# Ordering the three matmuls of a split product by parts in a one-core transformer kernel

## The chip, the cores and the metric

The kernel runs on one core of one Trainium2 chip. The metric is device time in microseconds (us); lower is better. Three runs of the kernel before gave 1061.06, 1062.39 and 1064.32 us, a median of 1062.39 us. The profile is of one more execution, which took 1064.48 us.

## The reference, cut to what matters

A sequence of 256 tokens with model width 1024 goes through seven layers, all in float32: differential attention with a pooling mixer, a feed-forward layer with a short convolution, sliding-window attention, a second such feed-forward layer, a SwiGLU layer, a mixer of a 31-tap convolution and forgetting attention, and another SwiGLU layer. Every layer has a norm ahead of it and a residual behind it. What costs the time are the matrix products:

```python
proj = rms_norm(x, norm_g) @ w_in           # 1024 x 2048, 1024 x 1280, 1024 x 2568
x = x + mix @ w_out                         # 1024 x 1024, three times
h = rms_norm(x, norm_g) @ w_up              # 1024 x 5632, four times
x = x + (jax.nn.silu(gate) * up) @ w_down   # 2816 x 1024, four times
```

## The kernel before

**Products.** A float32 product is made of three matmuls of a rounded type. Activations and weights are each split into a first part (the rounded value, "hi") and a rest ("lo", what rounding took away): first by first, first by rest, and rest by first are summed in PSUM. One *block* is 128 rows of the contraction (index `ko`). With two token halves (`tb`, 128 tokens each) the activations stand as `xT` with a hi and a lo part.

There are three helpers. `mm3` (line 254, matmuls on lines 256 to 258) has activations as the stationary operand and weights as the moving one; it is called block by block from `rows_mm` (line 327), which `Proj.half`, `FFN.lead`, `OutProj.part` and `keys_C` use, and from `FFN.down` (line 428). `mm_w` (line 473, matmuls on lines 475 to 477) has weights stationary and 256 tokens moving; `conv_in` (line 1002), `forget_sums` (1056) and `proj_qk` (1089) call it once for each of the eight blocks. `mm_both` (line 479, matmuls on 483 and 485) makes the up-products of the feed-forward layers; it already goes by parts and isn't touched.

**Weights.** A `Stream` (line 174) loads weight chunks of 128 x 2048 in a written order through two staging tiles `st`. ScalarE casts the first part `whi` in two pieces (line 203), VectorE subtracts the rest `wlo` in four pieces of 512 columns (line 207). Five chunks are held at once. The splits have a priority that is 400 places behind the program's place (`LATER`, line 194). A chunk's buffers come free when the last matmul that reads them is done.

**Activations.** `split_T` (line 269) makes `xT` from transposes: ScalarE writes hi (line 274), then VectorE lo (line 275).

**Order.** The program is unrolled in Python. The order of the calls at lines 698 to 761, 886 to 960 and 1153 to 1224 is written by hand: products, scores, transposes and residuals of the three mixer layers are interleaved there. The tile layer then orders each engine's instructions by priority (the place in the program, with offsets such as `LATER`, and `LATERC = 300` for the convolution's rows on VectorE) and by what is ready, and puts in the semaphores. Each engine executes its instructions in that order.

In the last mixer layer `conv_in(3)` (line 1172) is followed by `proj_qk(1, 2)`, `proj_qk(1, 1)`, `proj_qk(0, 2)` and more (1174 to 1183). `proj_qk(1, ...)` reads the last two weight chunks of the stream for this layer. The 31-tap convolution runs on VectorE as `Conv.rows` (line 1030, instructions of line 1036), and `f1.scores` (line 1180) needs VectorE for line 586.

Of the kernel before, what the change touches and what calls it, by code (L numbers as in the profile page):

```python
# [18 lines left out]
P = 128  # L19
S = 256  # L20
D = 1024
KD = D // P
FF = 2816
NF = FF // P
# [84 lines left out]
def block_kernel(ctx: ExitStack, tc: tile.TileContext, a: dict, out: bass.AP):  # L109
    nc = tc.nc  # L110
    V, A, T, G = nc.vector, nc.scalar, nc.tensor, nc.gpsimd
# [114 lines left out]
    W = Stream()  # L226
# [24 lines left out]
    srow = const.tile([P, 280], F32, name="srow")  # L251
    nc.sync.dma_start(out=srow, in_=a["srow"].to_broadcast([P, 280]))

    def mm3(o, l, r, first, last):

        T.matmul(o, l[0], r[0], start=first, stop=False)  # L256
        T.matmul(o, l[0], r[1], start=False, stop=False)  # L257
        T.matmul(o, l[1], r[0], start=False, stop=last)  # L258

    def cut(pair, *idx):  # L260
        return tuple(t[idx] for t in pair)

    def tok(tb):
        return slice(tb * P, (tb + 1) * P)
# [61 lines left out]

    def rows_mm(o, xT, tb, w, kos, first, last, n0=0, n=512):

        for i, ko in enumerate(kos):
            mm3(  # L330
                o[:, :n], cut(xT, slice(None), ko, tok(tb)),
                cut(w, slice(None), i, slice(n0, n0 + n)),
                first and i == 0, last and i == len(kos) - 1,
            )

    def v3(pair, k):
        return tuple(t.rearrange("p (k n) -> p k n", k=k) for t in pair)

    class OutProj:
# [6 lines left out]
        def part(self, tb, *kks):  # L346
            if tb not in self.accs:
                self.accs[tb] = [acc_t(f"op{tb}{n}") for n in range(2)]
            for kk in kks:
                w = v3(W.get(self.wname, kk), 2)  # L350
                for n in range(2):
                    rows_mm(self.accs[tb][n], self.mixT, tb, w, (2 * kk, 2 * kk + 1),
                            self.done[tb] == 0, self.done[tb] == 3, n * 512)
                self.done[tb] += 1
                W.used(self.wname, kk)

# [4 lines left out]
    class FFN:  # L361
# [66 lines left out]
        def down(self, p, tb):  # L428
            if self.accs is None:
                self.accs = [[acc_t(f"dn{b}{n}") for n in range(2)] for b in range(2)]  # L430
            w = v3(W.get(self.dn, p), 2)
            for n in range(2):
                for i in range(2):
                    g = tuple(self.gs[p][:, i, k, tok(tb)] for k in range(2))
                    mm3(self.accs[tb][n], g, cut(w, slice(None), i, slice(n * 512, (n + 1) * 512)),
                        p == 0 and i == 0, p == NF // 2 - 1 and i == 1)
            W.used(self.dn, p)

        def run(self, pre, post, before=None, led=()):
# [30 lines left out]
        def residual(self, tb):  # L470
            add_residual(tb, self.accs[tb], 0.5 if self.half else None)

    def mm_w(o, w, xT, ko, first, last):
        x = cut(xT, slice(None), ko, slice(0, S))
        T.matmul(o, w[0], x[0], start=first, stop=False)
        T.matmul(o, w[0], x[1], start=False, stop=False)
        T.matmul(o, w[1], x[0], start=False, stop=last)

    def mm_both(o, ws, xT):

# [25 lines left out]
    xT = new_T("xT")  # L506
# [255 lines left out]
    xT = norm.dst  # L762
# [200 lines left out]
    xT = nT  # L963
# [38 lines left out]
    def conv_in(j):  # L1002
        ag[j] = ps_t("ag").rearrange("p (s t) -> p s t", s=2)
        w = v3(W.get("w2", j), KD)
        for s in range(2):
            for ko in range(KD):
                mm_w(ag[j][:, s, :], cut(w, slice(None), ko, slice(s * P, (s + 1) * P)),
                     xT, ko, ko == 0, ko == KD - 1)
        W.free(("w2", j))

    class Conv:
# [44 lines left out]
    def forget_sums():  # L1056

        o = ps_t("fl")[:8, :S]
        for ko in range(KD):
            mm_w(o, cut(flw, slice(None), ko), xT, ko, ko == 0, ko == KD - 1)  # L1060
        z, cum = (tmp.tile([P, S], F32, tag="sl", name=n)[:8, :] for n in ("z", "cum"))
        e = tmp.tile([P, S], F32, tag="m", name="e")[:8, :]
        A.activation(z, o, AF.Identity, bias=PVs("fb")[:8, :])
        V.scalar_tensor_tensor(e, z, -1.0, z, ALU.mult, ALU.min)
        A.activation(e, e, AF.Exp)
        A.activation(e, e, AF.Ln, bias=1.0)
        V.scalar_tensor_tensor(z, z, 0.0, e, ALU.min, ALU.subtract)
        V.tensor_tensor_scan(cum, one[:8, :].to_broadcast([8, S]), z, 0.0, ALU.mult, ALU.add)
        crow, ncrow = (u288(n, F32R)[:, :S] for n in ("crow", "ncrow"))
        V.memset(crow.bitcast(F32), 0.0)  # L1070
        A.copy(crow[0:8, :], cum)
        V.tensor_tensor(crow[32:40, :], cum, crow[0:8, :].bitcast(F32), ALU.subtract)
        V.tensor_scalar(ncrow, crow.bitcast(F32), -1.0, None, ALU.mult)
        gates["k"], gates["q"] = crow, ncrow
# [13 lines left out]

    def proj_qk(s, b):
        o = ps_t("qk")  # L1090
        for ko in range(KD):
            mm_w(o[:, :S], cut(v3(W.get("w2", 4 + 2 * s + ko // 4), 4), slice(None), ko % 4, slice(b * P, (b + 1) * P)),
                 xT, ko, ko == 0, ko == KD - 1)
        A.activation((q2, k2)[s][:, b, :], o[:, :S], AF.Copy, scale=1.0 if s else -0.125)
        if b == 3:
            W.free(("w2", 4 + 2 * s), ("w2", 5 + 2 * s))
# [222 lines left out]
```

## Time and profile before

| | |
|---|---|
| median of three runs | 1062.39 us (1061.06 to 1064.32) |
| the profiled execution | 1064.48 us |
| its span, first to last instruction | 1062.6 us |
| outside the span | 1.9 us |
| TensorE (PE) matmuls | 1038.6 us busy, 98% of the span, 5862 instructions |
| TensorE weight loads (PEld) | 895.1 us, 84%, 5862 instructions |
| VectorE (DVE) | 779.4 us, 73% |
| ScalarE (ACT) | 620.5 us, 58% |
| mean granted TensorE clock | 0.997 |

A busy matmul row lasts longer than the distance to the next one, because matmuls are pipelined: the rate is read from the start times. Four long stretches (126 to 299, 399 to 571, 582 to 757 and 889 to 1055 us) are the feed-forward layers; the first stretch, 299 to 399 and 757 to 889 us are the three mixer layers.

### The profile page before, as it was taken

The page shows a single profiled execution, that of the slowest core. Times are in us where ns is not written, and L with a number is a line of the kernel's source. Part 1 is how long each engine was busy: PE and PEld are TensorE (multiplying, and loading weights), DVE is VectorE, ACT ScalarE, POOL GpSimd, SP SyncE. Part 2 cuts the span into 40 slices and gives each one's busy share as a digit, 9 for nine tenths or more (in the row PEclk, how much of TensorE's full clock was granted, in tenths as well). Part 3 has the DMA queues.
Part 4 walks back from the last instruction along what each step waited for, and adds up shares of the span by engine and source line. Part 5 has one row for each costly group of instructions (what it writes and reads, how often), then busy time and mean ns, then how long its engine had stood idle before and what let it go on. Part 6 is the DMA issues. An engine that isn't in the chain of part 4 may idle for free.

```text
span 1062.6 us, 15441 instructions
## 1 busy us (share of the span) xinstructions
PE 1038.6 (98%) x5862; PEld 895.1 (84%) x5862; DVE 779.4 (73%) x1678; ACT 620.5 (58%) x1105; POOL 32.0 (3%) x40
## 2 busy tenths in 40 slices
PE   5999999999999999999999999999999999999997
PEld 4778988888887898888889888888898889888885
DVE  5786789788867579888787666656799896656652
ACT  5584666667657457766665555554644556555542
POOL 1100000000021000000000000000000010000000
PEclk9999999999999999999999999999999999999999
DMA  6654555655452064665545655554613166655531
GB/s 254 247 197 159 178 179 204 212 198 199 157 180 96 25 227 151 214 219 200 195 163 182 214 185 193 198 187 171 214 64 120 41 218 220 216 172 192 191 119 40
DMA packets 28442, 185.69 MB, mean 175 GB/s; under 512 B 3280, under 2 KB 4176, under 8 KB 7120
## 3 DMA queue, kind: packets, MB, share of 16 engines
q1 hardware_dynamic: 28368, 184.71, 50.1%
q8 instruction: 46, 0.75, 0.3%
q14 instruction: 28, 0.23, 0.1%
HBM read 183.65 MB, written 1.05 MB: 174 GB/s over the span
## 4 chain that ended last, share of the span: by engine, by line
PE 90%; DVE 3%; DMA 3%; ACT 2%; issue 0%; POOL 0%; SPq 0%; POOLq 0%; ACTq 0%; DVEq 0%
PE up L483 26%; PE up L485 13%; PE dn L256 8%; PE dn L257 8%; PE dn L258 7%; PE sc L583 2%; DMA st<-in_w 2%; PE op L256 2%; PE op L258 2%; PE op L257 2%; PE proj L256 2%; PE proj L258 2%; DVE wlo L207 2%; PE proj L257 2%; PE lead L258 2%; PE lead L257 2%
## 5 line engine op out<-in xcount | busy, mean ns | idle before, releaser
L207 DVE TENSOR_TENSOR wlo<-st,whi 128x512 fp32r<-128x512 f32 x668 | 433.4, 685 | 157.7 <-ACT whi L203 157.0
L203 ACT CAST whi<-st 128x1024 fp32r<-128x1024 f32 x334 | 338.7, 1048 | 136.8 <-PE dn L258 29.8
L483 PE MATMUL up<-xT,whi 128*128 128x512 f32 x1216 | 304.6, 392 | 1.4 <-DVE c L413 1.4
L483 PEld LDWEIGHTS up<-xT,whi 128*128 128x128 f32 x1216 | 220.6, 189 | 42.7 <-issue 1.8
L485 PEld LDWEIGHTS up<-xT,wlo 128*128 128x128 f32 x1216 | 165.9, 190 | 11.9
L485 PE MATMUL up<-xT,wlo 128*128 128x256 f32 x1216 | 169.6, 282 | 0.0
L256 PE MATMUL dn<-whi,g 128*128 128x512 f32 x352 | 137.7, 391 | 0.0
L257 PE MATMUL dn<-wlo,g 128*128 128x512 f32 x352 | 137.4, 390 | 0.0
L258 PE MATMUL dn<-whi,g 128*128 128x512 f32 x352 | 137.0, 389 | 0.0
L490 ACT COPY h<-up 128x256 f32<-128x256 f32 x152 | 55.8, 367 | 65.8 <-PE up L485 65.7
L258 PEld LDWEIGHTS dn<-whi,g 128*128 128x128 f32 x352 | 66.1, 188 | 14.3 <-DVE g L426 0.3
L256 PEld LDWEIGHTS dn<-whi,g 128*128 128x128 f32 x352 | 66.2, 188 | 12.9 <-ACT g L425 0.2
L257 PEld LDWEIGHTS dn<-wlo,g 128*128 128x128 f32 x352 | 66.2, 188 | 12.2
L425 ACT CAST g<-m 128x256 fp32r<-128x256 f32 x88 | 35.5, 405 | 60.9 <-DVE m L421 60.8
L491 DVE TENSOR_TENSOR h<-up,h 128x256 f32<-128x256 f32 x152 | 63.4, 417 | 9.6 <-ACT h L490 9.6
L256 PE MATMUL lead<-whi,xT 128*128 128x256 f32 x192 | 55.2, 288 | 0.0
L258 PE MATMUL lead<-whi,xT 128*128 128x256 f32 x192 | 54.3, 283 | 0.0
L257 PE MATMUL lead<-wlo,xT 128*128 128x256 f32 x192 | 54.3, 283 | 0.0
L410 ACT ACTIVATE c<-h,pv 128x256 f32<-128x256 f32 x76 | 45.8, 603 | 6.7 <-DVE h L491 6.6
L256 PE MATMUL proj<-whi,xT 128*128 128x512 f32 x112 | 46.2, 412 | 2.3 <-ACT xT L274 2.3
L426 DVE TENSOR_TENSOR g<-m,g 128x256 fp32r<-128x256 f32 x88 | 36.9, 422 | 14.7 <-ACT g L425 11.8
L284 ACT ACTIVATE junk<-x 128x512 bf16<-128x512 f32 x32 | 20.2, 631 | 44.6 <-DVE x L323 26.0
(215 smaller groups left out, 1389.2 us busy)
## 6 DMA issues: line engine op xcount, KB each, us to landing
st<-in_up SPq DMA_DIRECT2D x88, 1024.0 KB, 4.8
st<-in_dn SPq DMA_DIRECT2D x44, 1024.0 KB, 4.8
st<-in_w SPq DMA_DIRECT2D x22, 1024.0 KB, 4.8
gb<-in_rows SPq DMA_DIRECT2D x10, 512.0 KB, 4.3
st<-in_w0o SPq DMA_DIRECT2D x4, 1024.0 KB, 5.0
st<-in_w1o SPq DMA_DIRECT2D x4, 1024.0 KB, 4.8
st<-in_w2o SPq DMA_DIRECT2D x4, 1024.0 KB, 4.9
st<-in_w SPq DMA_DIRECT2D x2, 512.0 KB, 7.0
```

The source lines that it names most:

```text
L203: A.copy(hi[:, c], st[:, c])
L207: V.tensor_sub(lo[:, c], st[:, c], hi[:, c].bitcast(F32))
L256: T.matmul(o, l[0], r[0], start=first, stop=False)
L257: T.matmul(o, l[0], r[1], start=False, stop=False)
L258: T.matmul(o, l[1], r[0], start=False, stop=last)
L410: A.activation(c, ps, AF.Identity, bias=PVs(cb, blk), scale=PVs(cw, 3 * blk + 2))
L425: A.copy(hi, m)
L426: V.tensor_sub(lo, m, hi.bitcast(F32))
L483: T.matmul(o, w[0], xT.both(ko), start=ko == 0, stop=False, skip_group_check=True)
L485: T.matmul(o[:, :S], w[1], xT[0][:, ko, :], start=False, stop=ko == KD - 1, skip_group_check=True)
L490: A.copy(h, o[:, S:])
L491: V.tensor_tensor(h, o[:, :S], h, ALU.add)
```

## The change

`mm3` takes a list of blocks and issues first by first for all of them, then the activations' rest by the weights' first, then the activations' first by the weights' rest. `mm_w` takes all eight blocks and issues first by first, first by the activations' rest, then the weights' rest. `OutProj.part` and `FFN.down` put both 512-column halves of the output into one list, except for the last chunk, where each half is still finished on its own. The matmuls, their operands and their number are the same; only their order changes.

```diff
-    def mm3(o, l, r, first, last):
-
-        T.matmul(o, l[0], r[0], start=first, stop=False)
-        T.matmul(o, l[0], r[1], start=False, stop=False)
-        T.matmul(o, l[1], r[0], start=False, stop=last)
+    def mm3(terms, first, last):
+
+
+        begun, left = set(), {}
+        for o, _, _ in terms:
+            left[id(o)] = left.get(id(o), 0) + 1
+        for i, j in ((0, 0), (1, 0), (0, 1)):
+            for o, l, r in terms:
+                end = j == 1 and left[id(o)] == 1
+                left[id(o)] -= j
+                T.matmul(o, l[i], r[j], start=first and id(o) not in begun, stop=last and end)
+                begun.add(id(o))
...
     def rows_mm(o, xT, tb, w, kos, first, last, n0=0, n=512):
 
-        for i, ko in enumerate(kos):
-            mm3(
-                o[:, :n], cut(xT, slice(None), ko, tok(tb)),
-                cut(w, slice(None), i, slice(n0, n0 + n)),
-                first and i == 0, last and i == len(kos) - 1,
-            )
+        o = o[:, :n]
+        mm3([(o, cut(xT, slice(None), ko, tok(tb)), cut(w, slice(None), i, slice(n0, n0 + n)))
+             for i, ko in enumerate(kos)], first, last)
...
-                for n in range(2):
-                    rows_mm(self.accs[tb][n], self.mixT, tb, w, (2 * kk, 2 * kk + 1),
-                            self.done[tb] == 0, self.done[tb] == 3, n * 512)
+                last = self.done[tb] == 3
+                for ns in ((0,), (1,)) if last else ((0, 1),):
+                    mm3([(self.accs[tb][n], cut(self.mixT, slice(None), 2 * kk + i, tok(tb)),
+                          cut(w, slice(None), i, slice(n * 512, (n + 1) * 512))) for n in ns for i in range(2)],
+                        self.done[tb] == 0, last)
...
-            for n in range(2):
-                for i in range(2):
-                    g = tuple(self.gs[p][:, i, k, tok(tb)] for k in range(2))
-                    mm3(self.accs[tb][n], g, cut(w, slice(None), i, slice(n * 512, (n + 1) * 512)),
-                        p == 0 and i == 0, p == NF // 2 - 1 and i == 1)
+            last = p == NF // 2 - 1
+            for ns in ((0,), (1,)) if last else ((0, 1),):
+                mm3([(self.accs[tb][n], tuple(self.gs[p][:, i, k, tok(tb)] for k in range(2)),
+                      cut(w, slice(None), i, slice(n * 512, (n + 1) * 512))) for n in ns for i in range(2)], p == 0, last)
...
-    def mm_w(o, w, xT, ko, first, last):
-        x = cut(xT, slice(None), ko, slice(0, S))
-        T.matmul(o, w[0], x[0], start=first, stop=False)
-        T.matmul(o, w[0], x[1], start=False, stop=False)
-        T.matmul(o, w[1], x[0], start=False, stop=last)
+    def mm_w(o, ws, xT):
+
+        for i, j in ((0, 0), (0, 1), (1, 0)):
+            for ko, w in enumerate(ws):
+                T.matmul(o, w[i], xT[j][:, ko, :], start=(i, j, ko) == (0, 0, 0), stop=i == 1 and ko == KD - 1)
...
-            for ko in range(KD):
-                mm_w(ag[j][:, s, :], cut(w, slice(None), ko, slice(s * P, (s + 1) * P)),
-                     xT, ko, ko == 0, ko == KD - 1)
+            mm_w(ag[j][:, s, :], [cut(w, slice(None), ko, slice(s * P, (s + 1) * P)) for ko in range(KD)], xT)
...
-        for ko in range(KD):
-            mm_w(o, cut(flw, slice(None), ko), xT, ko, ko == 0, ko == KD - 1)
+        mm_w(o, [cut(flw, slice(None), ko) for ko in range(KD)], xT)
...
-        for ko in range(KD):
-            mm_w(o[:, :S], cut(v3(W.get("w2", 4 + 2 * s + ko // 4), 4), slice(None), ko % 4, slice(b * P, (b + 1) * P)),
-                 xT, ko, ko == 0, ko == KD - 1)
+        mm_w(o[:, :S], [cut(v3(W.get("w2", 4 + 2 * s + ko // 4), 4), slice(None), ko % 4, slice(b * P, (b + 1) * P))
+                        for ko in range(KD)], xT)
```

## Rows read from the trace of the kernel before

**Rows 1.** The page, part 1: busy time, share of the span and instructions of each engine.

```profile
PE 1038.6 (98%) x5862; PEld 895.1 (84%) x5862; DVE 779.4 (73%) x1678; ACT 620.5 (58%) x1105; POOL 32.0 (3%) x40
```

**Rows 2.** The page, part 4: the chain that ended last, shares of the span.

```profile
PE 90%; DVE 3%; DMA 3%; ACT 2%; issue 0%; POOL 0%; SPq 0%; POOLq 0%; ACTq 0%; DVEq 0%
```

**Rows 3.** Stretches: length, busy PE, PEld, DVE, ACT, POOL; PEclk; DMA share, GB/s.

```profile
126.00:299.00 173.00, 172.54 (x916) 148.70 (x917) 146.75 (x307) 115.85 (x201) 2.17 (x3) 1.00 0.55 190
...
801.40:816.60 15.20, 15.20 (x107) 13.14 (x106) 14.68 (x39) 9.01 (x17) 0.00 (x0) 1.00 0.40 138
816.60:820.00 3.40, 3.40 (x17) 2.95 (x15) 2.21 (x11) 1.48 (x6) 0.00 (x0) 0.51 0.00 0
...
889.00:1062.60 173.60, 166.29 (x875) 142.89 (x873) 100.91 (x198) 86.40 (x146) 1.10 (x2) 0.99 0.47 161
```

**Rows 4.** What PE waited for: us in total, times, longest us.

```profile
PE ptx L497 <- DVE xn L300: 8.5, 1, 8.5
PE proj L256 <- ACT xT L274: 2.3, 3, 1.7
...
PE qk L477 <- DVE wlo L207: 1.2, 3, 0.5
```

**Rows 5.** PE's timeline in a feed-forward stretch: start us, us, engine, line, operation.

```profile
196.95 0.39 PE L258 MATMUL dn<-whi,g 128*128 128x512 f32 x1
197.17 0.39 PE L256 MATMUL dn<-whi,g 128*128 128x512 f32 x1
197.40 0.39 PE L257 MATMUL dn<-wlo,g 128*128 128x512 f32 x1
197.63 0.39 PE L258 MATMUL dn<-whi,g 128*128 128x512 f32 x1
197.85 0.39 PE L256 MATMUL dn<-whi,g 128*128 128x512 f32 x1
```

**Rows 6.** The page, part 5: the casts of the weights; idle time before them, what ended it.

```profile
L203 ACT CAST whi<-st 128x1024 fp32r<-128x1024 f32 x334 | 338.7, 1048 | 136.8 <-PE dn L258 29.8
```

**Rows 7.** PE's timeline where the first attention product reads the last weight chunks.

```profile
794.24 0.28 PE L476 MATMUL qk<-xT,whi 128*128 128x256 f32 x1
795.01 0.39 PE L477 MATMUL qk<-xT,wlo 128*128 128x256 f32 x1 [0.50 <-DVE wlo L207]
795.24 0.28 PE L475 MATMUL qk<-xT,whi 128*128 128x256 f32 x1
795.36 0.28 PE L476 MATMUL qk<-xT,whi 128*128 128x256 f32 x1
```

**Rows 8.** VectorE's timeline there: first and last of seven wlo pieces, then a score.

```profile
794.27 0.68 DVE L207 TENSOR_TENSOR wlo<-st,whi 128x512 fp32r<-128x512 f32 x1
...
800.05 0.68 DVE L207 TENSOR_TENSOR wlo<-st,whi 128x512 fp32r<-128x512 f32 x1
...
811.57 0.42 DVE L586 CUSTOM_DVE_ANT_0 S<-sc,cc 128x256 f32<-128x256 f32 x1
```

**Rows 9.** ScalarE's timeline: the copy out of the second of these products.

```profile
801.82 0.39 ACT L1094 ACTIVATE qk<-qk 128x256 f32<-128x256 f32 x1 [0.22 <-PE qk L477]
```

**Rows 10.** PE's timeline behind the last norm's transposes in the last mixer layer.

```profile
756.72 0.39 PE L257 MATMUL proj<-wlo,xT 128*128 128x512 f32 x1
756.95 0.51 PE L475 MATMUL ag<-xT,whi 128*128 128x256 f32 x3
757.47 0.50 PE L258 MATMUL proj<-whi,xT 128*128 128x512 f32 x1
```

**Rows 11.** PE's timeline behind the second norm of the first layer.

```profile
22.06 0.40 PE L257 MATMUL proj<-wlo,xT 128*128 128x512 f32 x1
22.76 0.50 PE L258 MATMUL proj<-whi,xT 128*128 128x512 f32 x1 [0.30 <-DVE xT L275]
```

**Rows 12.** The chain that ended last, from 22 to 52 us: start us, us, what.

```profile
27.99 4.92 DMA st<-in_w
...
50.39 1.17 ACT kTA L571 x2
```

## The prediction

> **What bounds the kernel now.** I read the busy times first: PE has a matmul in flight for 1038.6 us of a span of 1062.6 us, and there is one weight load for each matmul, 5862 of each [rows 1]. Then the chain of waits: 90% of it is PE, and the 8% of DVE, DMA and ACT are few pieces in the mixer layers [rows 2]. The stretch view says where PE is not full: a feed-forward stretch of 173.00 us has PE busy for 172.54 us [rows 3], so nothing that makes PE wait less can help there. Of the 24.0 us that PE is idle in all (1062.6 - 1038.6), 8.5 us lie ahead of its first transpose [rows 4] and 7.3 us behind its last matmul (173.60 - 166.29 in the last stretch) [rows 3]. So **8.2 us** of idle time are left in the middle, and only those can be won by an order that waits less.
>
> A full PE could still run at another rate, so I looked at the start times in a feed-forward stretch: a matmul of 512 columns starts every 0.22 or 0.23 us, whichever of the three it is [rows 5].
>
> **The change, part by part.** It neither adds nor removes a matmul, a load, a copy or a DMA. It moves 2712 matmuls within their groups (by the counts of lines 256 to 258 and 475 to 477 in the groups by line: 1056 of the down-products, 576 lead, 336 proj, 288 op, 48 kv, 192 qk, 192 ag, 24 fl). Each part has a price:
>
> 1. *The rate.* In the rows the step from line 256 to 257 keeps the stationary operand and takes 0.23 us, 257 to 258 changes it and takes 0.23 us, and 258 to 256 goes to another block and takes 0.22 us, before and after alike [rows 5]. The new order is made of the same steps in another mixture, so I cost it at nothing. The starts are shown to 0.01 us, and a mean over many such steps can't be off by more than some 1 ns: bounds of 2712 x 1 ns = 2.7 us either way.
>
> The Trainium skill ("TensorE: Matmul & The Clock Gate", section "Step-by-step: what each phase is for") says that loading is kept apart from computing so that one can load once and multiply repeatedly, which speaks against parting two matmuls with the same weights, as this change does. The trace does not show such a saving: there is a load for every matmul [rows 1].
>
> 2. *The wait for the weights' rest.* After `conv_in(3)`, the first `proj_qk` that uses the last two weight chunks stands still for the `wlo` pieces, because each block's third matmul needs one. The waits view has 1.2 us in three waits [rows 4]; by the starts the first one costs 0.77 us where a step takes 0.12 us, so 0.65 against the 0.50 that is listed, and the next step takes 0.23 us, another 0.11 [rows 7]. With that 0.26 on each of three the loss is 1.2 + 0.8 = 2.0 us. In the new order 16 of the 24 matmuls of a product need no `wlo`, 16 x 0.12 = 1.92 us of work from 793.8 on. The pieces still come one in 0.97 us (seven, from 794.27 to 800.05 + 0.68 = 800.73) [rows 8], since VectorE has convolution rows between them. The second product is copied out at 801.82 [rows 9]. If the two products that are interleaved there now share the first-part matmuls, they can't end ahead of 800.73 plus two matmuls, 801.0: a gain of 0.8 us. If a third product fills in as well, the full 2.0 us. Midway is 1.4 us on PE.
>
> What is late next is VectorE: from 801.40 to 816.60 it is busy for 14.68 of 15.20 us, and the first score of `f1.scores` starts at 811.57 with no wait ahead of it [rows 3, 8]. It comes out of VectorE's queue behind convolution rows, so a PE that is early stands in front of the same queue unless the tile layer also moves rows behind scores. I let half through: **-0.7 us**.
>
> 3. *The wait for the activations' rest.* Behind the norm's transposes at 756.7 the third matmul waits for `xT` lo: 0.75 us from 757 to 258, of which three `ag` matmuls that slip in fill 0.36 and the step itself takes 0.23 [rows 10]; 0.16 is lost, and 0.1 more on the next step. The new order has four first-by-first matmuls (0.9 us) ahead of it. PE is on the chain there: **-0.26 us**. In the first layer the same wait costs 0.70 - 0.23 = 0.47 us [rows 11]. There the chain goes not over PE but over weight loading and the copies behind it: a DMA of 4.92 us at 27.99, and at the end the ACT copy at 50.39 that PE waits for [rows 12]. An earlier PE waits longer for that: **0**, with 0.5 us as the bound.
>
> 4. *First parts needed sooner.* With all blocks' first parts in front, the second half of `whi` and the later blocks of `xT` hi are needed 2 to 3 times sooner. In `Proj`, `OutProj` and `down` a chunk is split at least a chunk ahead of its use, and the wait for `xT` hi, 2.3 us in three [rows 4], is of the first matmul in either order. I cost it at 0; the cover is the five chunks that the stream holds. If it is gone, a wait is one cast, 1.05 us [rows 6], at each of the three mixer layers: up to 3.1 us as a bound.
>
> 5. *Buffers.* The last reader of `whi` moves forward by 4 of 12 matmuls (0.9 us), of `wlo` back by one (0.23 us). ScalarE's casts wait 29.8 us in all for the down-products [rows 6] and so start earlier, but no matmul of a full stretch waits for them [rows 3]: 0. SP's queue, whose loads wait for staging tiles, gets no other work.
>
> Sum: -0.7 - 0.26 = -1.0 us. The profiled execution took 1064.5 us (1062.6 in the span, 1.9 around it), so its like would take 1063.5 us; it stood 2.1 us above the median of 1062.4 us, so the median goes to **1061.4 us**, -0.09%. A measurement of this kernel can tell about 0.3% (3.2 us) from no change.
>
> **The rivals.**
>
> - *VectorE or the weight stream takes all of it.* For it: no wait ahead of the first score, the chain of the first layer. Nothing passes, 1062.4 us. The same time comes out if the tile layer, which orders by what is ready, keeps PE close to its old order; that it does reorder is seen where three `ag` matmuls stand inside a `proj` product [rows 10].
> - *The layers' schedule gets better as a whole.* Less waiting for second parts lets scores and transposes come sooner, and the hand-written mixture fits better. For it: the waits are spread over the three mixer layers. Against it: the largest of them are for transposes, norms and weights, not for second parts. Of the 8.2 us of idle time in the middle, 1.7 us are the wait for the first `xT` of all [rows 4]; 6.5 us are left, which would give 1055.9 us. I put this case at 1057 us.
> - *Slower: the product holds the queue.* The place is the first `proj_qk` after `conv_in(3)`. PE executes in order: if its eight `wlo` matmuls stand ahead of the next product's first parts, it does 16 matmuls until 795.7 and then goes at the pace of the pieces until 800.73. The second product then takes 24 x 0.12 = 2.9 us and ends at 803.7 instead of 801.7: +2.0 us. That is decided by whether the next product's `whi` matmuls come ahead of those. PE would idle for some 4 of 5 us, and idling has a second price: from 816.60 to 820.00, behind scores with gaps, the granted clock was 0.51, near the lower level of 1.2 GHz, so 3.4 us did the work of 1.7 [rows 3]. One more such stretch is +1.7 us. Together 1062.4 + 3.7 = 1066.1 us. Against it: products are already interleaved there.
> - *Slower: the pairs with one stationary operand were worth something.* By the rule of the Trainium skill above, 904 pairs (768 in `mm3`, 136 in `mm_w`) would lose it. As a mechanism here: if the second of a pair were faster by the 0.01 us that the starts can't show, 904 x 0.01 = 9 us, 1071 us. The rows give both steps the same time [rows 5].
>
> **How the numbers follow.** My forecast, a small gain of 0 to 3 us, gets 0.54; nothing passes 0.10; the better schedule 0.24; the held queue 0.10; the pairs 0.02. Below 1059.2 us (faster by 0.3%) lie the better schedule's 0.24 and the edge of the forecast with the rate's bound, 0.03: 0.27. Above 1065.6 us lie most of the held queue and the pairs: 0.10. The rest, 0.63, is within 0.3%. The range leaves out half of the better schedule's low side and the far end of the slower cases: 1056.5 to 1065.5 us; the lower end is the forecast less the 2.7 us of the rate and part of the 6.5 us, the upper end adds the 3.1 us of early first parts.
>
> **What would show it.** In the profile of the changed kernel the feed-forward stretches should last 172 to 173 us again, with starts 0.22 to 0.23 us apart. The wait of `qk` for `wlo` should shrink from 1.2 us, that of `proj` for `xT` lo should be gone, and VectorE should be full from 790 to 816 us at its old times. The forecast is wrong if the rate changes in a full stretch, if a new wait for `whi` or `xT` hi of over 1 us shows, if the stretch at half clock is gone or comes twice, or if the mixer layers as a whole are more than 3 us shorter.

## The result and the profile after

Nine executions of the changed kernel have a median of 1072.76 us (1066.48 to 1083.74) against 1063.05 us for nine of the kernel before on the same chip; the ratio is **1.0064 [1.0047, 1.0080]**. The ratio leaves out the execution of 1083.74 us, which counts as a slow one; without it the median is 1070.90 us. The change makes the kernel slower; the forecast of 1061.4 us and its range were both too low. The profiled execution took 1068.0 us (span 1066.0 us), 3.5 us more than that of before.

The page after, parts 1 and 4, answers to [rows 1, 2]:

```profile
PE 1037.4 (97%) x5862; PEld 892.6 (84%) x5862; DVE 780.9 (73%) x1678; ACT 620.9 (58%) x1105; POOL 33.0 (3%) x40
PE 89%; DVE 4%; DMA 3%; ACT 2%; POOL 1%; issue 1%; SPq 0%; POOLq 0%; ACTq 0%; DVEq 0%
```

PE has the same 5862 matmuls and is busy for 1.2 us less, in a span that is 3.4 us longer: it waits more. The waits of PE after answer to [rows 4] (us in total, times, longest). Lines are shifted by 1 to 7; `mm3` is now the one line 264, `mm_w` line 482, and 483 of before, the up-product, is 488.

```profile
PE ptx L502 <- DVE xn L307: 9.4, 2, 9.2
PE up L488 <- ACT sl L425: 3.3, 2, 1.9
PE proj L264 <- ACT xT L281: 2.1, 3, 1.6
PE pt L502 <- DVE qkn L572: 1.5, 1, 1.5
PE pt L502 <- DVE z L1125: 1.2, 1, 1.2
PE qk L482 <- DVE wlo L207: 1.2, 2, 0.6
PE pt L502 <- DVE kn L801: 1.0, 1, 1.0
```

Two rows of before that [rows 4] leaves out:

```profile
PE up L483 <- DVE c L413: 1.4, 2, 1.1
PE pt L497 <- DVE z L1124: 0.6, 1, 0.6
```

`up` waits 3.3 us behind ScalarE's `sl`, where before it waited 1.4 us behind VectorE's `c`; the wait for `z` has doubled; the 1.0 us behind `kn` has no row before; `qk` loses as much to `wlo` as it did. The same view of stretches as [rows 3]: the first and third stand for those of before, the second lies behind the wait of 1.9 us, the fourth where before was at half clock.

```profile
125.30:298.30 173.00, 172.56 (x916) 148.71 (x917) 145.45 (x305) 114.41 (x199) 2.17 (x3) 1.00 0.54 186
401.29:404.71 3.42, 3.42 (x12) 2.73 (x11) 3.38 (x9) 3.15 (x7) 0.00 (x0) 0.50 0.01 2
805.10:820.30 15.20, 15.20 (x109) 13.33 (x108) 14.97 (x41) 8.63 (x17) 0.00 (x0) 1.00 0.36 129
820.30:823.70 3.40, 3.40 (x25) 2.96 (x24) 3.12 (x16) 2.12 (x10) 0.00 (x0) 1.00 0.02 5
```

The full stretch has the same busy time and the same 916 matmuls. One stretch at half clock has gone from the last mixer (820 us) and one has come at 401 us, where there was none.

To place the loss I cut each profiled execution into stages by start times in PE's timeline (us). The kernels of the other columns are those of the experiments below; "third profile" is another execution of the changed kernel, one of 1072.75 us, which the expectations call its third look.

| stage | before | changed | third profile | lead by block | release late | only lead | only x-proj |
|---|---|---|---|---|---|---|---|
| up to the first matmul | 8.49 | 9.19 | 9.25 | 9.44 | 9.31 | 8.99 | 9.12 |
| first layer, to the first `lead` | 94.43 | 92.75 | 93.18 | 94.48 | 94.86 | 94.13 | 95.34 |
| first feed-forward, `lead` to last `dn` | 187.98 | 188.29 | 188.48 | 187.34 | 187.38 | 190.07 | 187.20 |
| second mixer, last `dn` to `lead` | 85.46 | 86.34 | 86.37 | 86.37 | 85.44 | 85.44 | 86.32 |
| second feed-forward | 186.92 | 190.32 | 188.31 | 188.00 | 187.17 | 188.62 | 187.25 |
| third, and to the first `qk` | 216.23 | 216.40 | 216.36 | 216.34 | 215.92 | 216.23 | 216.18 |
| last mixer, `qk` to its last score | 54.82 | 53.20 | 59.19 | 65.99 | 56.31 | 54.82 | 54.06 |
| then to the last feed-forward's `lead` (the tail) | 35.35 | 36.53 | 36.54 | 36.53 | 35.26 | 35.28 | 36.50 |
| last feed-forward, end | 192.93 | 192.94 | 192.96 | 192.95 | 192.94 | 192.93 | 192.92 |

Three losses repeat in all four profiles of the changed kernel: at the starts of the two first feed-forwards, in the second mixer (+0.9 us), and in the last mixer's tail (+1.2 us). What differs from profile to profile is the last mixer up to its scores, and the second feed-forward.

### The profile page after: what moved, and what is told of

Read it like the earlier page. It is cut to its first block, busy times and chain, and to the rows that moved or that the text cites. A ratio compares the mean times of both kernels' runs of the same rounds, so it can differ in the third digit from the quotient of the medians.

```text
span 1066.0 us, 15463 instructions
## 1 busy us (share of the span) xinstructions
PE 1037.4 (97%) x5862; PEld 892.6 (84%) x5862; DVE 780.9 (73%) x1678; ACT 620.9 (58%) x1105; POOL 33.0 (3%) x40
## 3 DMA queue, kind: packets, MB, share of 16 engines
HBM read 183.65 MB, written 1.05 MB: 173 GB/s over the span
## 4 chain that ended last, share of the span: by engine, by line
PE 89%; DVE 4%; DMA 3%; ACT 2%; POOL 1%; issue 1%; SPq 0%; POOLq 0%; ACTq 0%; DVEq 0%
PE up L488 26%; PE dn L264 22%; PE up L490 13%; PE lead L264 6%; PE op L264 5%; PE proj L264 5%; PE sc L588 2%; PE qk L482 2%; DMA st<-in_w 2%; DVE wlo L207 2%; PE ag L482 2%; PE o L847 1%; PE ptx L502 1%; DMA st<-in_dn 1%; ACT whi L203 1%; PE pt L502 1%
## 5 line engine op out<-in xcount | busy, mean ns | idle before, releaser
L264 PE MATMUL dn<-whi,g 128*128 128x512 f32 x704 | 177.1, 391 | 0.0
L264 PEld LDWEIGHTS dn<-whi,g 128*128 128x128 f32 x704 | 129.5, 188 | 25.9 <-ACT g L431 0.6
L264 PE MATMUL dn<-wlo,g 128*128 128x512 f32 x352 | 95.4, 389 | 0.0
L264 PE MATMUL proj<-whi,xT 128*128 128x512 f32 x224 | 59.9, 406 | 2.1 <-ACT xT L281 2.1
L264 PE MATMUL op<-whi,mixT 128*128 128x512 f32 x192 | 53.2, 403 | 0.2 <-ACT mixT L281 0.2
L264 PEld LDWEIGHTS proj<-whi,xT 128*128 128x128 f32 x224 | 41.5, 193 | 12.2 <-ACT xT L281 3.0
L264 PE MATMUL lead<-whi,xT 128*128 128x256 f32 x384 | 51.0, 286 | 0.0
L264 PEld LDWEIGHTS lead<-whi,xT 128*128 128x128 f32 x384 | 47.8, 191 | 0.5 <-DVE xT L282 0.3
L1039 DVE SCALAR_TENSOR_TENSOR ys<-u,dwh,ys 128x240 f32<-128x240 f32 (+29 forms) x109 | 45.0, 464 | 0.2
```

The costliest lines, as they stand in the source:

```text
L264: T.matmul(o, l[i], r[j], start=first and id(o) not in begun, stop=last and end)
L1039: V.scalar_tensor_tensor(y[:, k:], self.u[:, :S - k], self.w(k), y[:, k:], ALU.mult, ALU.add)
```

## The experiments

Theory A: by parts, the last matmul that reads a chunk's `whi` comes earlier, so the buffer is free earlier, and the tile layer puts the cast of a later chunk (and VectorE's `wlo` pieces) further ahead in engines that execute in order, in front of small urgent work. Theory B: the order of the matmuls itself costs. Theory C: it is only the clock in the mixers. The experiments ran on several chips; each ratio compares with executions of the kernel before on the same chip.

### The lead products alone: back to blocks, and alone by parts

Lead by block, the changed kernel with this edit:

```diff
-                rows_mm(o[:, 2 * P * i:], self.xT, tb, v3(W.get(self.up, f), KD), range(KD), True, True, 0, 2 * P)
+                oo, w = o[:, 2 * P * i:2 * P * (i + 1)], v3(W.get(self.up, f), KD)
+                for ko in range(KD):
+                    x, wk = cut(self.xT, slice(None), ko, tok(tb)), cut(w, slice(None), ko, slice(0, 2 * P))
+                    T.matmul(oo, x[0], wk[0], start=ko == 0, stop=False)
+                    T.matmul(oo, x[0], wk[1], start=False, stop=False)
+                    T.matmul(oo, x[1], wk[0], start=False, stop=ko == KD - 1)
```

> The changed kernel, but the two lead products of each feed-forward go block by block again. Theory A (early release: by parts, the lead's last reader of a chunk's high parts comes earlier, so ScalarE's cast of a later chunk is queued between the two copies that follow the lead, waits there for its weights' DMA, and holds the gates): the cast stands behind both copies again, the first gate of the second feed-forward is on time, the second up product waits about 0.4 us where the changed kernel's waited 1.9, no half-clock stretch follows, the 32 up matmuls take 13.7 us in place of 16.9; time 1061 to 1065 us. Theory B (the order of the matmuls itself, wherever it is, mostly in the output projections and the down products): the time stays at 1067 to 1073 us. Theory C (the mixers' clock varies in the changed kernel, whatever the feed-forwards do): 1066 to 1073 us with further half-clock stretches inside a mixer.

Only lead, the kernel before with the opposite edit (three loops over `ko`: first by first, the activations' rest, the weights' rest):

> The kernel before, with nothing changed but the two lead products, which go by parts. Theory A: the second up product of the second feed-forward waits 1.5 to 2.5 us for ScalarE, a half-clock stretch of about 3.4 us may follow, the 32 up matmuls take 15 to 17 us; time 1065 to 1070 us. Theory B: 1061 to 1064 us, as before. Theory C: 1061 to 1064 us.

ScalarE's timeline at the start of the second feed-forward (start us, us, engine, line, operation, idle before and its releaser), first the kernel before, then the changed kernel, lead by block and only lead:

```profile
395.34 0.37 ACT L374 COPY lead<-lead 128x256 f32<-128x256 f32 x1 [0.61 <-PE lead L258]
...
397.26 0.56 ACT L410 ACTIVATE c<-up,pv 128x256 f32<-128x256 f32 x1 [1.08 <-DVE c L413]
```

```profile
395.54 0.37 ACT L380 COPY lead<-lead 128x256 f32<-128x256 f32 x1 [1.57 <-PE lead L264]
395.81 0.57 ACT L416 ACTIVATE c<-up,pv 128x256 f32<-128x256 f32 x1
397.54 1.05 ACT L203 CAST whi<-st 128x1024 fp32r<-128x1024 f32 x1 [1.17 <-DMA st<-in_dn]
398.50 0.56 ACT L416 ACTIVATE c<-up,pv 128x256 f32<-128x256 f32 x1
399.07 1.28 ACT L425 ACT_TABLE_LOAD   x1
400.37 0.42 ACT L425 ACTIVATE sl<-c 128x256 f32<-128x256 f32 x1
```

```profile
396.63 0.37 ACT L385 COPY lead<-lead 128x256 f32<-128x256 f32 x1 [0.62 <-PE lead L383]
396.90 0.57 ACT L421 ACTIVATE c<-up,pv 128x256 f32<-128x256 f32 x1
398.54 0.56 ACT L421 ACTIVATE c<-up,pv 128x256 f32<-128x256 f32 x1 [1.07 <-DVE c L424]
```

```profile
397.62 0.37 ACT L378 COPY lead<-lead 128x256 f32<-128x256 f32 x1 [0.21 <-PE lead L375]
397.93 0.57 ACT L414 ACTIVATE c<-up,pv 128x256 f32<-128x256 f32 x1
399.44 1.05 ACT L203 CAST whi<-st 128x1024 fp32r<-128x1024 f32 x1 [0.95 <-DMA st<-in_dn]
400.40 0.56 ACT L414 ACTIVATE c<-up,pv 128x256 f32<-128x256 f32 x1
```

With the lead by parts a weight cast stands between the two `c` copies. It first waits 1.17 us for the DMA of its staging tile, then takes 1.05 us, and the second `c` is issued 2.96 us behind the lead's copy (398.50 - 395.54) in place of 1.91 us in lead by block and 1.92 us before. The table load and `sl` come behind it, and PE's next up-product waits for `sl`. In the changed kernel the chain that ended last runs over just these: the DMA (until 397.52 us), the cast, `c`, the table load, `sl`, the up-product. PE's rows for it in lead by block and in only lead:

```profile
PE up L493 <- DVE c L424: 0.5, 2, 0.3
```

```profile
PE up L487 <- ACT sl L423: 4.1, 2, 2.4
```

0.5 us where the lead goes by blocks, 4.1 us where nothing but the lead goes by parts: the lead's order alone makes this wait. Only lead costs 1069.2 us, ratio 1.0057 [1.0035, 1.0078], inside what theory A gave and above what B and C gave. Lead by block measured 1068.18 us, ratio 1.0050 [1.0030, 1.0070]: theory A's 1061 to 1065 us was missed, and the time alone would fit B and C. The wait did go, and the first feed-forward took 187.34 us, but the other losses stayed. (Its profile is of the slowest of its twelve executions, 1079.28 us, with a long last mixer; its second feed-forward's 188.00 us hold a wait of 0.6 us for a `g` cast.)

### The last two rounds exchanged

Release late, the changed kernel with this edit in `mm3`, so that `whi` is read in the last round, as before:

```diff
-        for i, j in ((0, 0), (1, 0), (0, 1)):
+        for i, j in ((0, 0), (0, 1), (1, 0)):
             for o, l, r in terms:
-                end = j == 1 and left[id(o)] == 1
-                left[id(o)] -= j
+                end = i == 1 and left[id(o)] == 1
+                left[id(o)] -= i
```

> The changed kernel, with the last two of the three rounds exchanged in the shared three-matmul helper: first by first, then the high activations with the weights' rest last becomes first by first, first activations by weights' rest, then activations' rest by first weights, or the reverse, whichever has the high weights read last again. Theory A: the high weights are free as late as before, the cast stands behind both copies, the second up product's wait is about 0.4 us; time 1061 to 1065 us. Theory B: an order by parts is an order by parts: 1067 to 1073 us. Theory C: 1066 to 1073 us.

It measured 1065.59 us, ratio **1.0012 [1.0000, 1.0025]**: still by parts in every product, yet four fifths of the loss is gone. The second mixer (85.44 us) and the tail (35.26 us) are as before, the second feed-forward (187.17 us) within 0.3 us. That is theory A's case and not B's, though the median lies 0.6 us above A's range. What is left stands in the last mixer up to its scores, 56.31 us after 54.82 us: `qk` waits 2.1 us for `wlo` (1.2 us before), and a stretch at half clock of 3.4 us lies behind that wait (800.56 us) in place of the one at 816 us. VectorE's timeline in the second mixer shows the same mechanism on another engine, first the changed kernel, then release late:

```profile
302.77 0.69 DVE L813 TENSOR_TENSOR qn<-proj,rs 128x512 f32<-128x512 f32 x1 [1.76 <-POOL rs L535]
303.38 4.29 DVE L207 TENSOR_TENSOR wlo<-st,whi 128x512 fp32r<-128x512 f32 x7
307.59 0.28 DVE L525 TENSOR_REDUCE ss<-sq 128x2 f32<-128x128 f32 x1
307.79 0.68 DVE L207 TENSOR_TENSOR wlo<-st,whi 128x512 fp32r<-128x512 f32 x1
...
309.42 0.29 DVE L801 TENSOR_TENSOR kn<-kv,rs 128x128 f32<-128x128 f32 x1 [0.87 <-POOL rs L535]
```

```profile
304.13 0.69 DVE L813 TENSOR_TENSOR qn<-proj,rs 128x512 f32<-128x512 f32 x1 [1.76 <-POOL rs L535]
304.74 2.49 DVE L207 TENSOR_TENSOR wlo<-st,whi 128x512 fp32r<-128x512 f32 x4
307.14 0.28 DVE L525 TENSOR_REDUCE ss<-sq 128x2 f32<-128x128 f32 x1
...
308.50 0.29 DVE L801 TENSOR_TENSOR kn<-kv,rs 128x128 f32<-128x128 f32 x1 [0.87 <-POOL rs L535]
```

Behind `qn` the changed kernel does seven `wlo` pieces, then the sum that the key norm needs, and one more piece ahead of the next step; release late does four and none. From `qn` to `kn` it takes 6.65 us against 4.37 us, and PE's transposes wait 1.0 us for `kn`; here too the chain that ended last runs over the pieces, the sum and `kn`. The kernel before has the order of release late, and also 4.37 us (307.86 - 303.49):

```profile
304.10 2.49 DVE L207 TENSOR_TENSOR wlo<-st,whi 128x512 fp32r<-128x512 f32 x4
```

### Which products cost in the mixers

Only x-proj is the kernel before with the three rounds in `Proj` and the key-value product alone:

```diff
-            rows_mm(self.o, xT, self.tb, w, range(4 * h, 4 * h + 4), h == 0, h == 1)
+            rows_parts(self.o, xT, self.tb, w, range(4 * h, 4 * h + 4), h == 0, h == 1)
...
-        rows_mm(kv[tb][:, :256], xT, tb, v3(W.get("w1", 0), KD), range(KD), True, True, 0, 256)
+        rows_parts(kv[tb][:, :256], xT, tb, v3(W.get("w1", 0), KD), range(KD), True, True, 0, 256)
```

> The kernel before, with nothing changed but the mixers' projections by token block (query, key and value of the first, key-value and query of the second, values of the last), which go by parts. Theory A2 (what the second and the last mixer lose comes from these products' earlier release of the high weights): the second mixer takes 86.3 us from the end of its feed-forwards to the lead where the kernel before takes 85.5, and the DVE normalisation of the keys holds TensorE's transposes 1.0 to 1.2 us; the feed-forwards are as before; 1063.5 to 1066 us. Rival D2 (it comes from the output projections): 85.5 us, and 1061.5 to 1064 us.

The other is the kernel before with `OutProj.part` and `FFN.down` as in the change:

> The kernel before, with nothing changed but the output projections and the down products, by parts. Theory A2: the 114.64 us of a full feed-forward stretch stay 114.64, the second mixer stays at 85.4 to 85.5 us; 1062 to 1064.5 us, no change that can be measured. Rival D2: the second mixer takes 86.3 us and the last mixer's tail 36.5 in place of 35.3; 1063.5 to 1066 us.

Only x-proj: 1066.27 us, ratio 1.0027 [1.0014, 1.0040], 0.3 us above A2's range, with a second mixer of 86.32 us and a tail of 36.50 us. Its rows in the waits:

```profile
PE pt L503 <- DVE kn L802: 1.0, 1, 1.0
...
PE up L489 <- DVE c L419: 0.5, 2, 0.3
```

Out and down: 1064.81 us, 1.0016 [0.9992, 1.0040], second mixer 85.46 us, tail 35.18 us: no loss that can be told. The time alone would not decide: it lies 0.3 us above A2's range and inside D2's. The stages do. For the second mixer A2 holds and D2 falls: only x-proj has the seven `wlo` pieces and the one more, and 6.65 us from `qn` to `kn`, like the changed kernel.

For the last mixer neither is shown. Only x-proj's tail is 1.15 us longer, but the stage ahead of it is 0.76 us shorter (54.06 us), so 0.4 us are lost from the first `qk` to the last `lead` (90.56 us after 90.17 us). In the changed kernel half of the tail's 1.2 us is seen where VectorE makes `z`, on the chain that ended last. VectorE's rows behind the second `on`, before and changed:

```profile
841.01 0.14 DVE L1121 TENSOR_SCALAR ss<-ss 128x1 f32<-128x1 f32 x1
841.07 0.68 DVE L207 TENSOR_TENSOR wlo<-st,whi 128x512 fp32r<-128x512 f32 x1
```

```profile
843.18 0.68 DVE L207 TENSOR_TENSOR wlo<-st,whi 128x512 fp32r<-128x512 f32 x1
843.78 0.15 DVE L1122 TENSOR_SCALAR ss<-ss 128x1 f32<-128x1 f32 x1
843.84 0.68 DVE L207 TENSOR_TENSOR wlo<-st,whi 128x512 fp32r<-128x512 f32 x1
```

A `wlo` piece stands ahead of the small sum, and from `on` to `z` it takes 2.39 us in place of 1.80 us. All four profiles of the changed kernel and both of lead by block show that. Only x-proj doesn't, only the 256-column products (below) don't, and release late doesn't; but with every product released late (all late, below) the tail takes 37.10 us, with a wait of 1.4 us for `z`. So the queue is shown, and which product's release fills it there is not.

### The 256-column products and the last mixer's clock

Only the gates, forget sums, query and key by parts (the change to `mm_w` and its three calls, on the kernel before):

> The kernel before, with only the 256-column products of the convolution and linear-attention mixers by parts (gates, forget sums, query and key). Theory A: the feed-forwards are as before, with the up product's wait at 0.4 us; query and key's wait for the weights' rest is 0.6 us shorter, and if the half-clock stretch at 816 us goes, 1.8 us go with it: 1059.5 to 1063 us. Theory B: 1060 to 1063 us. Theory C (the mixers' clock varies with their order): 1064 to 1070 us, with a half-clock stretch inside a mixer that the kernel before does not have.

The changed kernel without that part:

> The changed kernel, but the 256-column products of the mixers (gates, forget sums, query and key) go block by block as before. Theory A1: the losses of the lead and of the two DVE queues stay (3.4 + 0.9 + 1.2 us), the long half-clock stretches of the last mixer go: 1066 to 1069.5 us median, none above 1075. Rival C1 (the clock of the last mixer falls because of what stands ahead of it in time, not because of these products): as the changed kernel, 1068 to 1074 us with some executions over 1075.

Release late without that part:

> The changed kernel with the high weights read last again (first by first, high activations by the weights' rest before the activations' rest by the high weights, or the reverse, so that the release of the high weights is as late as before) and with the mixers' 256-column products block by block. Theory A1: no cast between the copies, the feed-forward steps are 0.8 us shorter than before in the first and the same in the second, the second mixer at 85.4 us, the last mixer as before with at most one half-clock stretch: 1062 to 1064.5 us, not slower than before. Rival B (any order by parts costs): 1066 to 1070 us.

Only these: 1067.2 us, ratio 1.0035 [1.0009, 1.0062], the profiled one 1076.58 us; its feed-forwards and second mixer lose nothing (187.20, 186.96, 85.44 us), as theory A said too. The time, `qk`'s wait for `wlo` (1.3 us, not shorter) and the half clock in the mixer (below) meet theory C and not A. Without them: 1069.67 us, 1.0057 [1.0041, 1.0072], the highest 1071.4 us, with the lead's wait of 3.3 us and the 1.0 us of `kn` unchanged; A1's median was missed by 0.2 us, and a stretch at half clock among the scores was there as well (below), so leaving them out did not keep the clock up. Release late without them: 1064.75 us, 1.0011 [0.9997, 1.0026], no change that can be told, and theory A1's forecast but for 0.25 us.

### More profiles of the same kernels

The changed kernel three times more, and lead by block once more:

> The changed kernel once more, for more executions and a second profiled one. Theory A1 (the fixed losses are the two feed-forward starts, a DVE queue in the second mixer and one in the last; what varies is the clock of the last mixer): the profiled execution repeats the second up product's wait of 1.9 us, the second mixer at 86.3 us and the last mixer's tail at 36.5 us; executions near 1067 us have one half-clock stretch besides the first layer's, those near 1073 us have two or three more between 800 and 850 us. Rival B1 (the slower executions lose their time in the feed-forwards): the extra half-clock stretches lie between 120 and 300 or 395 and 570 us.

> The changed kernel with the lead block by block, a second look: Theory A1: the feed-forwards are without the wait (up step 9.2 us from its start, as in the first look); the last mixer is at full clock in this execution or has one stretch: 1065 to 1069 us; the second mixer again 86.4 us and the last mixer's tail 36.5 us. Rival C1: the long half-clock stretch from 818 to 843 us is there again, 1077 to 1080 us.

> The changed kernel, a third profiled execution. Theory A1: second up product's wait 2.0 us and a half-clock stretch behind it, second mixer 86.3 us; if the execution is near 1068 us there is no half-clock stretch between 806 and 850 us, if it is near 1073 us there are some 7 to 10 us of it there. Rival B1: near 1073 us the additional half-clock stretch lies in a feed-forward.

> As the third look: near 1068 us, one half-clock stretch at the second feed-forward's start and none between 806 and 850 us; near 1073 us, 7 to 10 us at half clock between 806 and 850 us (theory A1) or in a feed-forward (rival B1).

The further profiled executions of the changed kernel took 1069.3, 1072.75 and 1069.74 us. Six executions on the chip of the first have a median of 1072.61 us, ratio 1.0080 [1.0061, 1.0098]. The stretch view (columns as in [rows 3]) of the third profile, then of the fourth at the same places:

```profile
401.00:404.40 3.40, 3.20 (x18) 2.85 (x19) 3.22 (x9) 3.40 (x9) 0.00 (x0) 1.00 0.01 2
801.57:804.98 3.41, 3.41 (x17) 3.41 (x17) 3.41 (x10) 1.32 (x2) 0.00 (x0) 0.50 0.76 245
...
818.64:828.88 10.24, 10.24 (x42) 8.80 (x41) 6.61 (x27) 2.94 (x12) 0.00 (x0) 0.50 0.01 2
```

```profile
403.47:406.88 3.41, 3.41 (x13) 2.93 (x12) 3.37 (x10) 3.41 (x8) 0.00 (x0) 0.50 0.01 2
...
818.64:828.88 10.24, 10.24 (x64) 8.13 (x64) 9.81 (x38) 5.66 (x19) 0.00 (x0) 1.00 0.01 2
```

In all four profiles the second mixer takes 86.3 to 86.4 us and the tail 36.5 us, as A1 said. Near 1068 to 1070 us (three profiles) there is one half-clock stretch behind the late up-product and none among the scores; near 1073 us (one profile) there is one behind `qk`'s wait for `wlo` and 10.24 us among the scores, with 42 matmuls where the fourth profile does 64. There A1 was wrong in one point: it had a wait of 2.0 us and a stretch behind the up-product as well, and the wait was 1.5 us, with none. Nothing of it lay inside the feed-forwards beyond their starts, so B1 falls for this one execution. From the table: the second feed-forward takes 188.31 us without the half-clock stretch and 190.32 to 190.37 us with it. Of these 2.0 us 0.4 us are the longer wait (1.89 against 1.50 us); some 1.6 us are the stretch.

The stretch among the scores is not the change's own: before has it for 3.4 us [rows 3]. The same view of lead by block, of its second profile, of only the 256-column products (behind `qk`'s wait, then among the scores), and of the changed kernel without them:

```profile
817.56:844.87 27.31, 27.31 (x92) 20.88 (x91) 14.98 (x54) 9.56 (x35) 0.00 (x0) 0.50 0.00 1
```

```profile
819.43:829.67 10.24, 10.24 (x42) 8.80 (x41) 6.65 (x27) 2.92 (x12) 0.00 (x0) 0.50 0.01 2
```

```profile
798.63:802.04 3.41, 3.41 (x18) 3.41 (x18) 3.41 (x10) 0.93 (x2) 0.00 (x0) 0.50 0.80 267
815.70:843.00 27.30, 27.30 (x90) 20.98 (x91) 14.07 (x49) 8.92 (x31) 0.00 (x0) 0.50 0.00 1
```

```profile
819.23:826.06 6.83, 6.83 (x26) 5.50 (x25) 4.05 (x17) 2.34 (x10) 0.00 (x0) 0.50 0.00 0
```

One kernel shows 27.31 us in one execution and 10.24 us in another. Lead by block's second profiled execution, 1073.28 us, lay above A1's range and below C1's.

### What brings the clock's fall more often

The query and key products alone by parts, the gates alone, and the changed kernel with the rounds exchanged in both helpers:

> The kernel before, with nothing changed but the query and key products of the last mixer, by parts. Theory E1 (these bring the clock's fall, since they stand still for the weights' rest in one long stretch ahead of the scores): 4 to 7 of 12 executions below a mean clock of 0.996, median 1065.5 to 1068 us, a half-clock stretch behind the wait near 799 us or one of over 5 us among the scores. Rival E2 (the gates' products bring it): at most 3 of 12, 1062.5 to 1065 us.

> The kernel before, with nothing changed but the convolution's gate products and the forget sums, by parts. Theory E1: at most 3 of 12 executions below 0.996, 1062.5 to 1065 us, like the kernel before. Rival E2: 4 to 7 of 12, 1065.5 to 1068 us.

> The changed kernel, with the last two rounds exchanged in both helpers, so that every product goes by parts and reads the high weights last. Theory A3 (early release is what all of the loss comes from, the clock's too): 1063 to 1065 us and at most 3 of 12 executions below 0.996. Rival E3 (the clock falls because the products by parts wait for the rest of several chunks in one stretch, whichever round comes last): 1065.5 to 1070 us, 4 or more of 12 below 0.996, and query and key's wait for the weights' rest of 2 us or more.

Query and key: 1064.93 us, ratio 0.9988 [0.9953, 1.0022], 6 of 12 executions below a mean clock of 0.996. Gates: 1063.9 us, 0.9991 [0.9963, 1.0020], 1 of 12. All late: 1065.87 us, 1.0006 [0.9976, 1.0037], 2 of 12, `qk`'s wait for `wlo` 0.7 us. On this chip 8 of 29 executions of the kernel before were below 0.996 too, three of them at 0.986 and 1074 to 1077 us. The counts go E1's way, but 6 of 12 against 8 of 29 is little, and query and key's median is 0.6 us below E1's range and inside E2's. For the clock A3 fits, whose time was missed by 0.9 us. None of the three times can be told from that of before, so they settle nothing on the time. No version was found that beats the kernel before.

The profiles say more on E1. The profiled execution of query and key has the half clock at both places that E1 named, from 798.73 to 802.14 us behind the wait and for 27.31 us from 815.79 us on. Over all 17 profiles a stretch at half clock stands behind `qk`'s wait in 5 of the 10 whose query and key products go by parts, and in none of the 7 where they go by blocks. In four of the five one of 10.24 or 27.31 us among the scores follows, in release late none. It is not the only way in: lead by block has its 27.31 us without the first.

## Why the prediction was wrong, and where it was right

**The rate** (0, with 2.7 us as its bound) was right. The full stretch has 172.56 us of busy PE in 173.00 us [rows 3: 172.54], and the last feed-forward takes 192.94 us after 192.93 us. The Trainium skill says ("TensorE: Matmul & The Clock Gate", section "Step-by-step: what each phase is for") that one can load once and multiply repeatedly. By the prediction's rival that would have made parted pairs dearer. No stage with full PE shows it, so the rival of 1071 us falls; that the time came out near it is chance.

**The wait for the weights' rest** (-0.7 us) brought nothing, and it failed on PE already. PE's wait is 1.2 us again [rows 4]. By the starts of ScalarE's copies the three products that end there come 20.82, 22.33 and 25.14 us behind the first `qk`, before 21.71, 22.31 and 25.19 us; the first score comes 30.79 us behind it, before 30.84 us. So the first product gains 0.9 us, and the second, which should have gained 0.8 us or more, nothing. That is the time of the rival "VectorE takes all of it", at this place, but not its way: the second product's gain is lost before VectorE's queue. Only that the queue is full was named rightly: 14.97 of 15.20 us.

**The wait for the activations' rest** (-0.26 us at 757 us) is gone from the waits, but the stage up to `qk` is 216.40 us after 216.23 us, so it did not pass on. In the first layer it was said to be eaten by what comes behind: the wait for `qkn` grew from 1.1 to 1.5 us while that for `xT` lo went. (The first layer is 1.2 to 1.7 us shorter in the changed kernel's profiles; the same stage differs by 1.0 us among kernels that leave it as it was, so little of that can be put down to the order.)

**First parts needed sooner** (0, at most 3.1 us) was right: no wait of PE for `whi` shows in the changed kernel.

**Buffers** (0) is the step that failed. It said that ScalarE's casts start earlier and that no matmul of a full stretch waits for them. Both are true, and neither asks what stands *behind* such a cast. In the lead, whose eight blocks are one list, the last reader of `whi` moves by a whole round of eight matmuls, and the tile layer answers by putting the cast between the two `c` copies, where it waits for a DMA with the gates behind it. The prediction's "4 of 12 matmuls" is `Proj`'s; it did not look at the lead. On VectorE the same happens with the `wlo` pieces in the second mixer. Measured: +0.3 us in the first feed-forward, +1.4 us in the second without its half-clock stretch, +0.9 us in the second mixer, +1.2 us in the tail, 3.8 us in all, where the sum had 0. (The first is small because the profile before has a wait of 1.1 us of its own there; against lead by block it is 0.95 us.) The exchange of two rounds takes the feed-forwards' and the second mixer's part away with everything still by parts. For the tail a fuller VectorE queue is shown, its cause is not.

**The second price.** The rival "the product holds the queue" was nearest in kind: an idle PE, then 3.4 us at half clock, for 1066.1 us. Its place was wrong in three profiles of four: there the half clock comes behind the feed-forward's late product, at some 1.6 us. In the third it does come behind the `qk` product, and costs more than the rival had: the third profile stands 4.4 us above before from `qk` to the last score (59.19 - 54.82), the first 1.6 us below. The prediction read the stretch of [rows 3] as standing behind scores with gaps, as the price of an idle PE; the row ahead of it has PE busy for 15.20 of 15.20 us, so that is not shown there. By the mean clock, 10 of 17 executions of the changed kernel lie below 0.996, and 19 of 96 of the kernel before (4 of 27, 3 of 17, 4 of 23, 8 of 29 by chip). So of the 8 to 9 us (1070.90 against 1063.05 us, 1072.61 against 1063.29 us) some 4 us are the queues, and by the third profile most of the rest is the clock. That profile adds up, stage by stage: 0.76 - 1.25 + 0.50 + 0.91 + 1.39 + 0.13 + 4.37 + 1.19 + 0.03 = 8.0 us over the profile before. The prediction named a half-clock stretch that goes or comes twice as a sign that it is wrong, but priced the clock as one event in a rival of 0.10; it should have been a term of the range, since [rows 3] already showed such a stretch in the last mixer.

**Left open:** why the last mixer's clock falls more often. The kernels that release `whi` late (release late, the same without the 256-column products, all late) have 5 of 36 executions below 0.996; those with `Proj` by parts and early release (changed, without the 256-column products, lead by block, only x-proj) have 28 of 48. But `Proj` is not all of it: the others that release early have 2 of 6 (only lead), 3 of 12 (out and down), 5 of 10 (only the 256-column products), 6 of 12 (query and key) and 1 of 12 (gates). The counts are from several chips and prove no cause. Nor do the parts add up: alone, lead, x-proj, the 256-column products, and out and down cost 0.57, 0.27, 0.35 and 0.16%, 1.35% together, where the change costs 0.64 to 0.80%.

## What to carry to other kernels

When an order moves the last reader of a buffer, follow the refill that this releases: which in-order queue it is now put into, which small instructions stand behind it there, and whether it still waits for something of its own, such as a DMA. If the order by parts is wanted, let the last round be the one that reads the buffer with the costly refill; exchanging two rounds here took back four fifths of the loss (a ratio of 1.0012 in place of 1.0064, on two chips). Where a profile shows a stretch at half clock, take several profiles before pricing anything: those of the changed kernel lie up to 4.75 us apart, and the first of lead by block stands 11 us above that kernel's median.

## What the runs showed of the hardware that was not expected

At the start of the second feed-forward the clock fell in three profiles of the changed kernel, where the up-product started 2.05 to 2.13 us late by the start times, and in the changed kernel without the 256-column products (2.02 us late), and not in the third (1.67 us late). In the profile of only lead the product of the first feed-forward was 2.59 us late and the clock stayed up; so the length of the wait alone does not decide. Once at half clock the last mixer stays there for 3.4, 6.8, 10.2 or 27.3 us, with PE shown busy all the time. The Trainium skill ("TensorE: Matmul & The Clock Gate", section "What's actually happening") says of a kernel's start that the number of matmuls at the lower level differs from run to run of one kernel. The two profiles of lead by block, 10.24 and 27.31 us, show the like in the middle of a kernel.
